# A gate matrix kept in HBM between two stages: its layout turned from piece first to group first

## The chip, the cores and the metric

The kernel runs on one core of one Trainium2 chip. The metric is the device time of one execution in microseconds (us); lower is better. The core has a matrix engine (PE), a vector engine (DVE), a scalar engine (ACT), GpSimd (POOL) and SyncE (SP), and sixteen DMA engines that all of them share. SP and ACT issue plain DMAs, each on a queue of its own (q1 is SP's, q10 is ACT's); POOL issues the indirect gathers (q0).

## The reference, cut to what matters

One encoder layer over 512 tokens of width 2048: attention and a recurrence, then a channel mixer (PEER) that picks, for each token, 16 experts from each of 8 heads out of 128 x 128 single-neuron experts. The change touches the mixer alone:

```python
out = lax.map(expert_chunk, ...)        # 128 tokens at a time
def expert_chunk(args):
    xc, ic, gc = args                   # tokens, 128 expert indices each, 128 gates each
    uc = u_emb[ic]
    act = jax.nn.gelu(jnp.einsum('cd,ced->ce', xc, uc))
    vc = v_emb[ic]
    return jnp.einsum('ce,ced->cd', (gc * act).astype(vc.dtype), vc)
```

## The kernel before, in words

176 of the 512 tokens are worked out by gathering rows of `u_emb` and `v_emb` (indirect DMAs on POOL, products on DVE, one "tick" at a time, spread over the whole mixer). The other 336 tokens (`TD`) are worked out densely: every expert's activation for every token, times a gate that is zero where the expert was not picked. The 16384 experts stand in 128 blocks (`NBLK`) of 128, one expert of a block to a partition.

The dense part has three steps.

- `u_block(b)` (lines 1118 to 1134) multiplies a block of `u_emb` with the tokens on PE (48 matmuls, in three products of high and low parts), takes the gelu on ACT into `ga`, 128 x 336, and stores most of these blocks to HBM (`ad`, line 1132). Its weights come as `raw` (1 MB by SP, line 255), are rounded to `hi` on ACT (line 269), and `lo = raw - hi` is made on DVE (line 281).
- While the first u blocks run, `g_step` builds the gates: 84 steps of four tokens, each a one-hot product on PE into `ps_G`, copied by ACT into `stg` (128 partitions x 128 blocks x 28 tokens, two buffers, line 1240). When 28 tokens (`TB`) are full, ACT writes the piece to the HBM matrix `gd` (line 1242): 12 pieces (`NTB`) in all, 14336 bytes of each partition.
- Later `load_g(g)` on SP (line 1341) reads back what a group of four blocks (`GRP`) needs, for all 336 tokens: 32 groups (`NG`), 5376 bytes of each partition. `weigh(b)` (lines 1343 to 1356) multiplies `ga` by its slice of `G` on DVE (line 1347), splits it into `Wh` and `Wl`, asks for the group after next, and reloads a stored `ga` as `gr` (line 1336, three buffers). `v_unit` then multiplies `Wh` and `Wl` with `v_emb` on PE (lines 1397 to 1399), eight blocks at a time; u blocks and v units alternate.

The order on every engine is written out by hand (`stage_plan`, `runs`); nothing is moved by a scheduler. An engine works through its instructions in order, and SP and ACT issue DMAs from the same streams, so a DMA that can't be issued yet holds up what stands behind it. Each DMA of SP and ACT counts its landing on one of eight counters (`DMAHW0` to `DMAHW7` in the built program), in turn; a DMA whose counter was last used by a transfer that may still be under way waits for that transfer first.

At one place ACT issues eight small loads in a row: `load_x` fetches the tokens of the last gather phase as `xng`, 16 partitions at a time (line 1148).

Of the kernel before, what the change touches and what calls it, by code (L numbers as in the profile page):

```python
# [8 lines left out]
F32 = mybir.dt.float32  # L9
# [21 lines left out]
NBLK = 128  # L31
GRP = 4
NG = NBLK // GRP
# [7 lines left out]
TB = 28  # L41
NTB = TD // TB
# [3 lines left out]
NB = 4  # L46
# [100 lines left out]
def tile_encoder(  # L147
# [24 lines left out]
    nc = tc.nc  # L172
    V, A, P, T = nc.vector, nc.scalar, nc.gpsimd, nc.tensor

    def pool(name, bufs=1, side="left", **kw):
        es = ExitStack()
        p = es.enter_context(tc.tile_pool(name=name, bufs=bufs, side=side, reuse_waits="tile", **kw))
        ctx.callback(es.close)
        return p, es.close
# [10 lines left out]
    psB = ctx.enter_context(tc.tile_pool(name="psB", bufs=2, space=PSUM))  # L190
    psC = ctx.enter_context(tc.tile_pool(name="psC", bufs=2, space=PSUM))
    dram = ctx.enter_context(tc.tile_pool(name="dram", bufs=1, space=DRAM))
    gd = dram.tile([128, NTB, NBLK, TB], F32, name="gd")
    x2d = dram.tile([DW, D], F32, name="x2d")
    x0d = dram.tile([128, D], F32, name="x0d")
    xnd = dram.tile([128 + NB1, D], F32, name="xnd")
# [461 lines left out]
    _, ps = next(gen)  # L658
# [160 lines left out]
    for c in range(4):  # L819
        ps = ps_l0 if c == 0 else [psA.tile([128, 512], F32, tag="A", name=f"ps_l{tt}") for tt in range(NT)]  # L820
# [391 lines left out]
    As, Bs, evac, gst = {}, {}, [], {}  # L1212
# [7 lines left out]
    def g_onehots(n):  # L1220

        if n < len(G_STEPS):
            tm, ta = G_STEPS[n]
            As[n] = g_one(lts[tm], ta, 0)
            if n % 2 == 0:
                V.tensor_tensor(As[n], As[n], lts[tm][:, 2, ta:ta + NB].unsqueeze(2).to_broadcast([128, NB, 128]),
                                op=ALU.mult)
        n -= 1
        if 0 <= n < len(G_STEPS):
            tm, ta = G_STEPS[n]  # L1230
            Bs[n] = g_one(lts[tm], ta, 1)
            if n % 2:
                for t in range(NB):
                    A.activation(out=As[n][:, t, :], in_=As[n][:, t, :], func=AF.Copy,
                                 scale=lts[tm][:, 2, ta + t:ta + t + 1])

    def flush_evac(keep=1):
        while len(evac) > keep:
            stg, o, ps, dst = evac.pop(0)
            A.copy(stg[:, :, o:o + NB], ps.rearrange("p t i -> p i t"))  # L1240
            if dst is not None:
                A.dma_start(out=dst, in_=stg)

    def g_step(n):
        flush_evac()
        g_onehots(n + G_AHEAD + 1)
        tt, ta = G_STEPS[n]
        B, Ao = Bs.pop(n), As.pop(n)
        at, o = divmod((tt - 1) * 128 + ta - NB1, TB)
        if o == 0:  # L1250
            gst["stg"] = gst["p"].tile([128, NBLK, TB], F32, tag="stg", name="stg")
        ps = psA.tile([128, NB, 128], F32, tag="A", name="ps_G")
        for t in range(NB):
            T.matmul(ps[:, t, :], B[:, t, :], Ao[:, t, :], start=True, stop=True)
        evac.append((gst["stg"], o, ps, gd[:, at] if o + NB == TB else None))

    def soft_b(t0):
        softmax_b(t0)
# [36 lines left out]
    def free_rt():  # L1295
# [6 lines left out]
    do = {"pair": lambda _: route_pair(), "sum": lambda _: route_sum(), "tr": lambda _: route_tr(), "sc": lambda _: route_sc(),  # L1302
          "pick": lambda _: route_pick(), "soft_a": lambda t: softmax_a(t, (1, 2, 4)[t]),
          "soft_b": soft_b, "free": lambda _: free_rt(), "g": g_step, "tick": lambda _: step(),
          "prime": lambda _: next(gg), "rep": lambda _: rep_lists(), "pre": g_onehots, "lists": lambda t: lts.update({t: g_lists(t)})}

    flush_lo()
    psS[:] = [psA, "A"]
    for b in range(lead0 - N_TRANS):
# [5 lines left out]

        u_block(b, hook)
    flush_evac(0)
    gst["close"]()
    gst["oh_close"]()
# [5 lines left out]
    gp, _ = pool("G", bufs=2)  # L1325
    grp, _ = pool("gr", bufs=3)
    acc = accp.tile([128, KD, TD], F32, name="acc")
    Gs, Ws = {}, {}
# [8 lines left out]

    def load_g(g):
        if g < NG:
            Gs[g] = gp.tile([128, NTB, GRP, TB], F32, tag="G", name="G")  # L1340
            nc.sync.dma_start(out=Gs[g], in_=gd[:, :, g * GRP:(g + 1) * GRP, :])

    def weigh(b):
        G, j = Gs[b // GRP], b % GRP
        ga = back_t.pop(b) if b in back_t else acts.pop(b)
        ga3 = ga.rearrange("p (a t) -> p a t", t=TB)
        V.tensor_tensor(ga3, ga3, G[:, :, j, :], op=ALU.mult)  # L1347
        Wh = wp.tile([128, TD], F32R, tag="Wh", name="Wh")
        Wl = wp.tile([128, TD], F32R, tag="Wl", name="Wl")
        A.copy(Wh, ga)  # L1350
        V.tensor_tensor(Wl, ga, Wh.bitcast(F32), op=ALU.subtract)  # L1351
        Ws[b] = Wh, Wl
        if j == GRP - 1:
            load_g(b // GRP + 2)
        if b in ad_at:
            reload()
# [21 lines left out]
    for i in range(N_TRANS):  # L1378
        ws = ((), (), (), range(3), range(3, 6), range(6, PR + LEAD))[i]
        u_block(lead0 - N_TRANS + i, beside=lambda: beside(ws))  # L1380
        if i == 0:
            for _ in range(3):
                reload()
        if i == 1:
            load_g(0)
            load_g(1)
# [205 lines left out]
```

## Time and profile before

| | |
|---|---|
| median of 3 runs | 2978.55 us (2971.44 to 2978.85) |
| the profiled execution | 2979.9 us, span 2978.1 us |
| PE busy in the span | 2849.8 us, 96% |
| DVE busy | 2321.1 us, 78% |
| ACT busy | 1145.4 us, 38% |
| DMA packets | 174624, of which 64096 are under 512 bytes |

"Busy" counts instructions of an engine from start to end; PE is busy nearly throughout, so what can be gained or lost shows in the time in which PE waits, stage by stage. The DMA share is the mean busy share of the sixteen DMA engines. The span is 1.8 us shorter than the time of the same execution.

### The profile page before, as it was taken

The numbers are of one execution on the slowest core, as the hardware profiler recorded it, in microseconds if no ns is written. First come the engines' busy times: TensorE is split into PE (matmuls) and PEld (weight loads), VectorE is DVE, ScalarE is ACT, GpSimd is POOL, SyncE is SP. The second block draws the span as 40 slices with busy tenths as digits, with TensorE's granted clock in tenths as the row PEclk, the third lists the DMA queues.
The fourth block names the chain that finished last, engine by engine and source line by source line (L and its number), as shares of the span: only waits on it lengthen the run. The fifth ranks groups of instructions, "written<-read, shape, count | busy, mean of one in ns | idle before, by whom it ended". The sixth has DMA issues, their size and how long they took to land. (4 is left out here: it accounts for less than half of the span.)

```text
span 2978.1 us, 41791 instructions
## 1 busy us (share of the span) xinstructions
PE 2849.8 (96%) x16945; PEld 2648.3 (89%) x16945; DVE 2321.1 (78%) x3206; ACT 1145.4 (38%) x1518; POOL 867.3 (29%) x562
## 2 busy tenths in 40 slices
PE   8999999999999999999999999999999999799997
PEld 6777867787889999998999999999999999799997
DVE  5773366544987899987888888888888888688885
ACT  6663254433444455543322232232333233232333
POOL 0000110001543422224343344344343433333322
PEclk9999999999999999999999999999999999999999
DMA  6222220233225798999999999999999999899983
GB/s 247 77 88 82 93 114 29 71 120 120 83 99 217 261 350 338 347 348 381 374 364 353 377 380 357 365 366 362 359 377 369 362 373 362 314 369 357 377 312 134
DMA packets 174624, 806.12 MB, mean 271 GB/s; under 512 B 64096, under 2 KB 82288, under 8 KB 83840
## 3 DMA queue, kind: packets, MB, share of 16 engines
q1 hardware_dynamic: 108096, 379.63, 34.4%
q0 software_dynamic: 52624, 379.42, 33.1%
q10 hardware_dynamic: 13712, 44.40, 4.0%
q8 instruction: 133, 2.18, 0.3%
q14 instruction: 59, 0.48, 0.0%
HBM read 759.33 MB, written 44.06 MB: 270 GB/s over the span
## 5 line engine op out<-in xcount | busy, mean ns | idle before, releaser
L281 DVE TENSOR_TENSOR lo<-raw,hi 128x2048 fp32r<-128x2048 f32 x316 | 724.4, 2293 | 380.9 <-ACT hi L269 379.6
L269 ACT CAST hi<-raw 128x2048 fp32r<-128x2048 f32 x316 | 603.4, 1910 | 739.2 <-PE ps_v L1398 464.0
L1399 PE MATMUL ps_v<-Wh,lo 128*128 128x336 f32 x2048 | 654.2, 319 | 26.5 <-DVE lo L281 26.5
L1397 PE MATMUL ps_v<-Wh,hi 128*128 128x336 f32 x2048 | 650.4, 318 | 20.4 <-DVE acc L1409 16.2
L299 PE MATMUL ps_u<-H,lo 128*128 128x336 f32 x2048 | 650.3, 318 | 10.1 <-DVE lo L281 10.0
L297 PE MATMUL ps_u<-H,hi 128*128 128x336 f32 x2048 | 653.5, 319 | 1.7 <-ACT hi L269 1.7
L1398 PE MATMUL ps_v<-Wl,hi 128*128 128x336 f32 x2048 | 650.8, 318 | 0.5
L298 PE MATMUL ps_u<-L,hi 128*128 128x336 f32 x2048 | 649.0, 317 | 0.0
L1154 POOL DMA_INDIRECT gv<-in_v_emb_dram,idx x176 | 351.3, 1996 | 582.1 <-DVE x L1181 426.3
L1154 POOL DMA_INDIRECT gu<-in_u_emb_dram,idx x176 | 333.5, 1895 | 631.4 <-DVE gu L1161 547.5
L1399 PEld LDWEIGHTS ps_v<-Wh,lo 128*128 128x128 f32 x2048 | 389.1, 190 | 29.4 <-DVE lo L281 29.3
L1397 PEld LDWEIGHTS ps_v<-Wh,hi 128*128 128x128 f32 x2048 | 389.5, 190 | 23.9 <-issue 18.3
L1161 DVE SCALAR_TENSOR_TENSOR gu<-gu,xng 128x2048 f32<-128x2048 f32 x176 | 400.8, 2283 | 2.4 <-DMA gu<-in_u_emb_dram,idx 2.4
L299 PEld LDWEIGHTS ps_u<-H,lo 128*128 128x128 f32 x2048 | 387.3, 189 | 12.6 <-DVE lo L281 12.6
L1398 PEld LDWEIGHTS ps_v<-Wl,hi 128*128 128x128 f32 x2048 | 389.1, 190 | 1.4 <-DVE Wl L1351 1.4
L297 PEld LDWEIGHTS ps_u<-H,hi 128*128 128x128 f32 x2048 | 387.7, 189 | 2.3 <-ACT hi L269 2.3
L298 PEld LDWEIGHTS ps_u<-L,hi 128*128 128x128 f32 x2048 | 387.6, 189 | 0.0
L1181 DVE SCALAR_TENSOR_TENSOR x<-gv,w,x 128x2048 f32<-128x2048 f32 x143 | 335.2, 2344 | 4.9 <-DMA gv<-in_v_emb_dram,idx 4.6
L1130 ACT ACTIVATE ga<-ps_u 128x336 f32<-128x336 f32 x128 | 57.5, 449 | 174.9 <-PE ps_u L299 174.4
L297 PE MATMUL ps_cm<-xh,hi 128*128 128x512 f32 x256 | 104.8, 409 | 11.5 <-ACT xh L368 9.2
L1409 DVE TENSOR_TENSOR acc<-ps_v,acc 128x336 f32<-128x336 f32 x240 | 109.6, 497 | 5.0 <-PE ps_v L1399 5.0
L1350 ACT CAST Wh<-gr 128x336 fp32r<-128x336 f32 x71 | 33.6, 473 | 193.8 <-DVE gr L1347 193.8
(321 smaller groups left out, 3678.5 us busy)
## 6 DMA issues: line engine op xcount, KB each, us to landing
raw<-in_u_t_dram SPq DMA_DIRECT2D x128, 1024.0 KB
raw<-in_v_t_dram SPq DMA_DIRECT2D x128, 1024.0 KB
raw<-in_w_dram SPq DMA_DIRECT2D x28, 1024.0 KB
gd<-stg ACTq DMA_DIRECT2D x12, 1792.0 KB
G<-gd SPq DMA_DIRECT2D x32, 672.0 KB
raw<-in_w_out_dram SPq DMA_DIRECT2D x16, 1024.0 KB
raw<-in_w_pq_dram SPq DMA_DIRECT2D x16, 1024.0 KB
ad<-ga ACTq DMA_DIRECT2D x71, 168.0 KB
```

What stands on the lines that cost most here:

```text
L269: A.copy(hi, raw)
L281: en.tensor_tensor(lo[:, c], raw[:, c], hi.bitcast(F32)[:, c], op=ALU.subtract)
L297: T.matmul(ps, ah, bh, start=first, stop=False)
L298: T.matmul(ps, ah, bl, start=False, stop=False)
L299: T.matmul(ps, al, bh, start=False, stop=last)
L1154: P.indirect_dma_start(out=g, out_offset=None, in_=u_emb if kind == "u" else v_emb, in_offset=bass.IndirectOffsetOnAxis(ap=ix, axis=0))
L1161: V.scalar_tensor_tensor(out=g, in0=g, scalar=1.0, in1=xs_t["x"], op0=ALU.mult, op1=ALU.mult, accum_out=a_t[h][:, k:k + 1])
L1181: V.scalar_tensor_tensor(out=d, in0=g, scalar=wk, in1=d, op0=ALU.mult, op1=ALU.add)
L1397: T.matmul(ps[:, 0:TD], hi[:, cc], Wh, start=j == 0, stop=False)
L1398: T.matmul(ps[:, 0:TD], hi[:, cc], Wl, start=False, stop=False)
L1399: T.matmul(ps[:, 0:TD], lo[:, cc], Wh, start=False, stop=j == PR - 1)
L1409: V.tensor_tensor(d, ps[:, 0:TD], d, op=ALU.add)
```

## The change

The HBM matrix `gd` has its axes in another order. Before, a partition's 14336 bytes of a piece were one run, and the 5376 bytes of a group were 12 runs of 448 bytes. Now a group's 5376 bytes are one run, and a piece goes into 32 runs of 448 bytes.

```diff
-    gd = dram.tile([128, NTB, NBLK, TB], F32, name="gd")
+    gd = dram.tile([128, NG, NTB, GRP * TB], F32, name="gd")
...
             if dst is not None:
-                A.dma_start(out=dst, in_=stg)
+                A.dma_start(out=dst, in_=stg.rearrange("p (g j) t -> p g (j t)", j=GRP))
...
-        evac.append((gst["stg"], o, ps, gd[:, at] if o + NB == TB else None))
+        evac.append((gst["stg"], o, ps, gd[:, :, at, :] if o + NB == TB else None))
...
-            Gs[g] = gp.tile([128, NTB, GRP, TB], F32, tag="G", name="G")
-            nc.sync.dma_start(out=Gs[g], in_=gd[:, :, g * GRP:(g + 1) * GRP, :])
+            Gs[g] = G = gp.tile([128, NTB, GRP, TB], F32, tag="G", name="G")
+            nc.sync.dma_start(out=G.rearrange("p a j t -> p (a j t)"), in_=gd[:, g].rearrange("p a f -> p (a f)"))
```

The tiles in SBUF keep their shapes, and no instruction of PE, DVE or POOL moves. On ACT, where a piece has been filled in the g steps, the issue stands at the same place and has another shape (`hi` is the rounded weight, `ohA` a one-hot operand):

```order
 L269 CAST hi<-raw 128x2048
 L1240 COPY stg<-ps_G 128x128x4
-L1242 DMA gd<-stg 128x3584
+L1242 DMA gd<-stg 4096x1x112
 L1234 ACTIVATE ohA<-ohA,lt 128x128 x4
 L1240 COPY stg<-ps_G 128x128x4 x2
```

One issue of 128 rows of 3584 elements has become one of 4096 rows of 112 elements; nothing around it moved. On SP, where the dense part changes from u blocks alone to u blocks and v units, the first loads of `G` stand among the weight loads and the reloads of `ga`:

```order
 L1336 DMA gr<-ad 128x336 x3
 L255 DMA raw<-in_u_t_dram 128x2048
-L1341 DMA G<-gd 128x12x112 x2
+L1341 DMA G<-gd 128x1344 x2
 L255 DMA raw<-in_v_t_dram 128x2048 x2
 L1336 DMA gr<-ad 128x336 x3
 L255 DMA raw<-in_v_t_dram 128x2048
-L1341 DMA G<-gd 128x12x112
+L1341 DMA G<-gd 128x1344
```

Again the shape alone differs. On ACT at the eight `xng` loads, with the counters that an issue waits for, four of the waits stay as they were and one is new, on the second load:

```order
-L1148 DMA xng<-xnd 16x2048 x4
+L1148 DMA xng<-xnd 16x2048
+L1148 DMA xng<-xnd 16x2048 [waits DMAHW5_49]
+L1148 DMA xng<-xnd 16x2048 x2
 L1148 DMA xng<-xnd 16x2048 [waits DMAHW0_49]
 L1148 DMA xng<-xnd 16x2048 [waits DMAHW1_49]
 L1148 DMA xng<-xnd 16x2048 [waits DMAHW2_49]
 L1148 DMA xng<-xnd 16x2048 [waits DMAHW3_49]
```

In both programs `DMAHW2` was last used by the `G` load that SP issues just before these loads, `DMAHW1` by the weight load ahead of it, and `DMAHW5`, in the changed program, by the `G` load of the group before that.

## Rows read from the trace of the kernel before

**Rows 1.** Page, part 1: busy us, share of span, instructions by engine
```profile
PE 2849.8 (96%) x16945; PEld 2648.3 (89%) x16945; DVE 2321.1 (78%) x3206; ACT 1145.4 (38%) x1518; POOL 867.3 (29%) x562
```

**Rows 2.** Windows by stage: length, PE, PEld, DVE, ACT, POOL busy, PEclk, DMA, GB/s
```profile
1050.00:1320.00 270.00, 257.10 (x1818) 255.00 (x1817) 260.13 (x278) 143.68 (x284) 63.91 (x41) 0.99 0.91 343
1340.00:2065.00 725.00, 688.11 (x4374) 681.16 (x4373) 616.47 (x553) 223.21 (x211) 285.49 (x135) 0.98 0.97 367
2065.00:2490.00 425.00, 423.75 (x2766) 423.50 (x2765) 372.70 (x315) 131.96 (x113) 165.84 (x85) 1.00 0.96 369
2490.00:2600.00 110.00, 95.06 (x609) 94.81 (x608) 81.97 (x70) 29.83 (x26) 37.67 (x19) 0.94 0.91 333
```

**Rows 3.** Waits, 1330 to 2110 us: total us, times, longest us
```profile
PE ps_v L1399 <- DVE lo L281: 26.5, 10, 4.0
...
DVE gr L1347 <- DMA gr<-ad: 18.3, 9, 2.7
```

**Rows 4.** DMA, 1617 to 1618 us: packets by size, then q1's packets, MB, share
```profile
DMA packets 699, 0.34 MB, mean 340 GB/s; under 512 B 674, under 2 KB 698, under 8 KB 698
...
q1 hardware_dynamic: 692, 0.32, 111.5%
```

**Rows 5.** DMA, 1060 to 1067 us: q10 with one write to gd
```profile
q10 hardware_dynamic: 144, 1.84, 61.3%
```

**Rows 6.** DMA, 1082.7 to 1088.4 us: q10 with the next write to gd
```profile
q10 hardware_dynamic: 139, 1.84, 88.8%
```

**Rows 7.** Issues of gd's loads and writes: duration ns min/median/max, first and last start
```profile
L1341 SPq DMA_DIRECT2D G<-gd x32: 529/530/4172, 1334.5 to 2778.3; - x32
L1242 ACTq DMA_DIRECT2D gd<-stg x12: 326/326/327, 1056.4 to 1317.9; - x12
```

**Rows 8.** Timeline of SP at two places: start us, length us, issue
```profile
1334.49 5.20 SPq L1341 DMA_DIRECT2D G<-gd  x2
1339.79 8.13 SPq L255 DMA_DIRECT2D raw<-in_v_t_dram  x2
...
1610.80 0.53 SPq L1341 DMA_DIRECT2D G<-gd  x1
1611.84 4.89 SPq L1336 DMA_DIRECT2D gr<-ad  x1
```

**Rows 9.** Timeline of ACT at two of the twelve writes
```profile
1174.55 0.33 ACTq L1242 DMA_DIRECT2D gd<-stg  x1
...
1175.46 0.33 ACTq L1132 DMA_DIRECT2D ad<-ga  x1
1175.83 1.92 ACT L269 CAST hi<-raw 128x2048 fp32r<-128x2048 f32 x1 [0.40 <-ACT ga L1130]
...
1198.18 0.33 ACTq L1242 DMA_DIRECT2D gd<-stg  x1
1208.33 0.33 ACTq L1132 DMA_DIRECT2D ad<-ga  x1
```

**Rows 10.** Timeline of DVE at the first of these writes
```profile
1178.60 2.28 DVE L281 TENSOR_TENSOR lo<-raw,hi 128x2048 fp32r<-128x2048 f32 x1
```

**Rows 11.** Timelines of SP, ACT and DVE at the xng loads, then PE's longest wait
```profile
2526.30 0.53 SPq L1341 DMA_DIRECT2D G<-gd  x1
...
2550.79 1.30 ACTq L1148 DMA_DIRECT2D xng<-xnd  x2
2552.19 1.90 ACT L269 CAST hi<-raw 128x2048 fp32r<-128x2048 f32 x1 [22.55 <-issue]
...
2554.12 2.29 DVE L281 TENSOR_TENSOR lo<-raw,hi 128x2048 fp32r<-128x2048 f32 x1 [17.51 <-ACT hi L269]
...
PE ps_v L1397 <- DVE acc L1409: 14.9, 1, 14.9
```

**Rows 12.** DMA, 2537.6 to 2548.4 us, by queue
```profile
q0 software_dynamic: 426, 3.15, 80.0%
q1 hardware_dynamic: 732, 0.33, 15.4%
```

## The prediction

> **What bounds the kernel now.** I read the page's busy times first. PE is busy for 2849.8 of 2978.1 us [rows 1], so about 128 us is all that any change of transfers can give back, and more can be lost. The windows by stage show where those us lie. While the gates are built and written, 1050 to 1320 us, PE is busy for 257 of 270 us and DVE for 260: both are nearly full, and the DMA engines have a share of 0.91. From 1340 to 2065 us, where `G` is read and `ga` is reloaded, PE misses 37 us and DMA is at 0.97. From 2065 to 2490 us `G` is still read by the same small runs, DMA is at 0.96, and PE misses 1.3 us. From 2490 to 2600 us PE misses 15 us [rows 2]. So a slow `G` load alone costs nothing: the waits belong to the reloads and to one place near 2550 us.
>
> Then the waits. In the read stage PE waits 26.5 us for `lo`, because DVE, which makes it, waits 18.3 us in nine pieces for `gr` [rows 3]. At 2550 us the chain is longer, and starts at a `G` load. SP issues it at 2526.3. ACT's last two `xng` issues come out only at 2550.79, and `hi`, which stands behind them in ACT's stream, starts at 2552.19 after 22.55 us without work; DVE's `lo` waits 17.51 us for that `hi`, and PE 14.9 us for DVE [rows 11]. The issue that is let go at 2550.79 is the one that waits for `DMAHW2`, the `G` load's counter.
>
> **What the change removes and adds.** The count of 448-byte packets stays the same: 32 loads x 1536 = 49152 before, 12 writes x 4096 = 49152 after. They move from SP's queue to ACT's, and from the read stage to the write stage.
>
> *Price of a packet.* In the one us in which nearly only `G` packets ran, q1 took 111.5% of 16 engines for 692 packets: 17.84 us / 692 = 25.8 ns each [rows 4]. A write to `gd` is 128 packets of 14336 bytes: 61.3% of 16 x 7 us over at most these is 536 ns each, 4.3 us of all sixteen engines [rows 5]; the next took 88.8% of 16 x 5.7 us, 5.1 us [rows 6]. No row shows a 448-byte write; the reads of that size are the nearest rows, and I take their price. A write then costs 4096 x 25.8 / 16 = 6.6 us, 1.9 more than the mean of 4.7, or 23 us for twelve. A `G` load costs 2.5 us now; as 128 packets of 5376 bytes, by bytes at 536 ns for 14336, 201 ns each, 1.6 us. That is 0.9 less, 28 us for 32.
>
> *Gain at 2550 us: 11 us, plus 1.* Between 2537.6 and 2548.4 us q0 moved 426 packets and q1 732 [rows 12], so in ten us the `G` load passed less than half of its 1536 small packets: it gets about one or two turns for each gather packet of 8192 bytes. With 128 packets instead of 1536 it needs a twelfth of these turns and should land before 2540 us. ACT is then let go some 11 us earlier. The bounds are 0 (another of the eight waits takes over) and 14.9. One us more comes back because the granted clock, 0.94 of the 2.4 GHz level in this stretch [rows 2], falls around such a wait. The Trainium skill says the same of the turns ("DMA: Bandwidth & Descriptors", Queues, rings and completion order: each DMA engine goes round its queues packet by packet); the count in rows 12 agrees.
>
> *Gain in the read stage: 5 us.* After a `G` load the next issue on SP is held: 4.89 us behind one [rows 8], where an issue of 128 rows takes 0.33. That hold goes, since 8 packets an engine replace 96. But the reload that DVE waits for mostly stands ahead of the `G` load in SP's stream, behind a 1 MB weight load, and the stage stays full of gathers. I give back 0.9 us less DMA work at about half a dozen of the stalls. Bounds: 0, and the 18.3 us of the nine waits.
>
> *Loss on ACT in the write stage: 17 us.* The write puts 256 packets on each engine where a `G` load put 96. Behind one `G` load the next issue came out 5.9 us after the load's own issue (1610.80 to 1616.73); with two `G` loads in a row the second was itself held (4172 ns instead of 530, [rows 7]), and the weight load behind them came out some 13 us after the first issue [rows 8]. So the issue of `gd` may pass, but the next one on ACT, `ad<-ga`, will be held until part of the 256 packets has gone. ACT's queue has no weight loads ahead of it: the last 160 packets an engine are 160 x 25.8 ns = 4.1 us, and with the start of the transfer at least 5 us; the two loads in a row, scaled to 256 packets, give 17 us. I take 8, nearer to the emptier queue. In the twelve writes `ad` comes from 0.91 us (the issue at 1174.55) to 10.15 us (at 1198.18) behind `gd` [rows 9]; taking 8 less each gap, the holds add up to 25 us. Behind `ad` stands `hi`, and DVE, which is full, takes up `lo` as little as 0.85 us after `hi` has ended (1177.75 to 1178.60, [rows 9, 10]). After the slack of each block some 17 us are left as DVE waits. Bounds by the same sum: 5 us of waits at 5 us a write, 70 at 13.
>
> *Loss to full DMA engines: 5 us.* Twelve writes add 23 us to a stage whose engines are idle for 0.09 x 270 = 24 us [rows 2]. It just fits; gathers and weights are asked for early, so I charge a fifth. Bounds 0 and 23. The last write lands later too; SP's first reload waits for it, and the two `G` loads behind, no longer held for 5.20 us [rows 8], give that back.
>
> **Sum.** -11 - 1 - 5 + 17 + 5 = +5 us on the profiled execution's 2979.9, so 2985. That execution lies 1.4 us above the median of the runs shown, which gives 2983.5 there; I say 2984. A difference under 0.3%, 9 us, can't be told from none.
>
> **Rivals.**
> - *The writes are hidden: 2963.* If ACT's queue takes 256 packets an engine without holding the next issue, only the gains remain: 2980 - 17. For it: every `gd` issue now takes 326 ns and none is held [rows 7]. Against it: the same queue type on SP does hold. It decides when `ad` still takes 0.33 us.
> - *ACT is held by the write itself: about 3010.* If the issue of `gd` can't complete until its packets fit, as the second `G` load's did not [rows 7], ACT loses 6 to 7 us at each of twelve places, of which it now idles about half before the next `hi`; the same sum gives 22 to 45 us of DVE waits instead of 17.
> - *Small writes cost more than small reads: about 3040.* If each 448-byte write takes twice its 25.8 ns, a write costs 13 us, DMA work grows by 12 x 8.5 = 100 us where 24 are free, and the stage lengthens by some 75 us; less the gains, 60 remain. In the trace nothing speaks for it and nothing excludes it. The Trainium skill gives such a rule ("DMA: Bandwidth & Descriptors", Specifications: 512 bytes are the least for full rate, and below it the DMA engine reads, modifies and writes); no run here shows a write that small. By that rule, this rival is the outcome.
> - *In between: about 2995.* Write packets of 30 to 36 ns add 14 to 31 us to a DMA stage that is then over-full.
>
> **How the numbers follow.** The sum as it stands, within 9 us of before: 0.32. Hidden writes, or a larger gain at the reloads: 0.24. ACT held by the write itself: 0.18. Dearer writes in between: 0.14. Twice the price: 0.12. So faster 0.24, same 0.32, slower 0.44. The range runs from 2957 (both gains near their bounds, no loss) to 3040 (the third rival), and leaves out about 2 in 10. The likeliest case alone: 2970 to 2989.
>
> **What would show it.** In the profile after: `ad<-ga` issues longer than 0.33 us behind `gd` show the hold, a `gd` issue of several us shows the second rival, and q10's share over one write shows the packet's price. DVE's busy time from 1050 to 1320 us and the waits of `lo` for `hi` there show what the holds cost. No issue on SP held behind a `G` load, and PE's 14.9 us wait cut to about 4, show the gains. The prediction is wrong if small writes have another price than small reads, or if the hold isn't set by packets that are still queued.

## The result and the profile after

The changed kernel takes 2995.28 us (median; 2994.4 to 3006.51 in 4 runs), the kernel before 2977.03 us on the same chip: a ratio of 1.0075, 95% interval 1.006 to 1.009, so 18 us slower. The profiled execution of after is the longest of its four (3006.51 us; the others lie between 2994.4 and 2995.75), so sums of its trace come out some 11 us above the medians.

The windows by stage, with the columns of [rows 2], of the kernel after:

```profile
1050.00:1320.00 270.00, 240.36 (x1629) 235.58 (x1627) 238.95 (x258) 129.07 (x259) 51.20 (x36) 0.96 0.91 305
1340.00:2065.00 725.00, 690.26 (x4392) 682.92 (x4391) 612.28 (x538) 223.00 (x207) 280.92 (x135) 0.98 0.96 369
2065.00:2490.00 425.00, 420.07 (x2723) 419.55 (x2722) 369.71 (x317) 132.34 (x118) 167.30 (x84) 0.99 0.94 363
2490.00:2600.00 110.00, 99.70 (x634) 99.45 (x633) 87.04 (x73) 31.50 (x30) 42.31 (x20) 0.94 0.95 340
```

The loss is in the first line, where the gates are written: PE is busy for 17 us less than in [rows 2] and DVE for 21 us less, POOL for 13 us less, and the clock is at 0.96 instead of 0.99, while the DMA share, 0.91, is the same: the DMA engines have not become fuller, and PE and DVE wait for something else. The read stage gains 2 us of PE and the place at 2550 us 4.6. The windows stand at the same times in both traces, and behind the write stage the work comes some 28 us later in this one, so what a stage loses at its end can fall into the next. Of the 3.7 us that the third line loses, most is such a shift: PE's last wait of the read stage, 2.8 us for `lo`, ends at 2089.36 us, where one of 3.2 ended at 2061.48 before. The rest belongs to a wait that ends at 2371.97 us, 2.1 us where it was 1.3.

The issues of the writes, of `G` and of `ad` (duration ns min/median/max, first and last start), after:

```profile
L1242 ACTq DMA_DIRECT2D gd<-stg x12: 520/521/582, 1053.2 to 1344.5; - x12
L1341 SPq DMA_DIRECT2D G<-gd x32: 319/386/606, 1364.2 to 2804.8; - x32
L1132 ACTq DMA_DIRECT2D ad<-ga x71: 321/326/10008, 880.0 to 2004.6; - x71
```

No write is held when it is issued, and no `G` load is held any more (4172 ns at most in [rows 7]). From the first to the last write 291.3 us pass; before it was 261.5 us (1056.4 to 1317.9, [rows 7]). And one `ad`, 168 KB, took 10 us to issue. The timeline of ACT around it, after, and DVE's and PE's at the same place:

```profile
1181.55 0.53 ACTq L1242 DMA_DIRECT2D gd<-stg  x1
1182.18 0.45 ACT L1130 ACTIVATE ga<-ps_u 128x336 f32<-128x336 f32 x1 [0.66 <-ACT stg L1240]
1182.67 10.01 ACTq L1132 DMA_DIRECT2D ad<-ga  x1
1192.72 1.90 ACT L269 CAST hi<-raw 128x2048 fp32r<-128x2048 f32 x1 [10.08 <-issue]
```
```profile
1194.65 2.29 DVE L281 TENSOR_TENSOR lo<-raw,hi 128x2048 fp32r<-128x2048 f32 x1 [8.96 <-ACT hi L269]
```
```profile
1194.67 0.65 PE L297 MATMUL ps_u<-H,hi 128*128 128x336 f32 x1 [5.10 <-ACT hi L269]
1195.11 0.48 PE L298 MATMUL ps_u<-L,hi 128*128 128x336 f32 x1
1196.99 0.65 PE L299 MATMUL ps_u<-H,lo 128*128 128x336 f32 x1 [1.40 <-DVE lo L281]
```

This is the whole chain in one place: the write passes in 0.53 us, the small `ad` behind it stands for 10 us, `hi` behind `ad` comes after 10.08 us without work ("issue": ACT waited for nothing but its own stream), DVE stands 8.96 us and PE 5.10 and 1.40 us. PE then pays again. In these windows (columns as before) its granted clock is 0.50 and 0.54, the 1.2 GHz level, after the wait, and 1.00 before it and eight us later:

```profile
1180.00:1189.50 9.50, 9.50 (x68) 9.29 (x66) 5.65 (x8) 1.97 (x6) 1.16 (x1) 1.00 1.08 302
1194.60:1199.00 4.40, 2.94 (x9) 2.51 (x10) 4.35 (x2) 4.00 (x9) 0.00 (x0) 0.50 0.31 51
1199.00:1203.00 4.00, 4.00 (x17) 4.00 (x16) 3.96 (x7) 2.11 (x6) 1.16 (x1) 0.54 0.98 377
1203.00:1207.00 4.00, 4.00 (x34) 4.00 (x33) 4.00 (x4) 1.51 (x4) 2.19 (x1) 1.00 0.38 160
```

In four us at 0.54 PE begins 17 matmuls, at 1.00 it begins 34. So, by an estimate from these counts, a 5 us wait costs some 4 us more: in the 8.4 us after it PE begins 26 matmuls, which take 3.1 us at the rate of 34 in four us, and waits 1.4 us.

`ad` is held by over 2 us behind seven of the twelve writes between 1084 and 1323 us (6.95, 6.16, 3.97, 10.01, 6.62, 7.60 and 6.18 us) and behind the last one, at 1350.42 (9.02 us), together 56.5 us. The waits from 1050 to 1345 us, after (total us, times, longest):

```profile
ACT hi L269 <- issue: 48.0, 7, 10.1
DVE lo L281 <- ACT hi L269: 33.6, 8, 9.0
```

In the kernel before, no `ad` was held, and `lo` waited 9.0 us for `hi` in three pieces (1050 to 1330 us):

```profile
L1132 ACTq DMA_DIRECT2D ad<-ga x71: 326/326/333, 883.2 to 1977.9; - x71
DVE lo L281 <- ACT hi L269: 9.0, 3, 6.1
```

### The profile page after: what moved, and what is told of

Same layout as the page of the kernel before. It is cut to its first block, busy times and chain, and to the rows that moved or that the text cites. A ratio compares the mean times of both kernels' runs of the same rounds, so it can differ in the third digit from the quotient of the medians.

```text
span 3004.7 us, 41792 instructions
## 1 busy us (share of the span) xinstructions
PE 2861.9 (95%) x16945; PEld 2658.0 (88%) x16945; DVE 2321.8 (77%) x3206; ACT 1144.9 (38%) x1518; POOL 863.9 (29%) x562
## 3 DMA queue, kind: packets, MB, share of 16 engines
q10 hardware_dynamic: 61328, 44.40, 5.2%
## 5 line engine op out<-in xcount | busy, mean ns | idle before, releaser
L1399 PE MATMUL ps_v<-Wh,lo 128*128 128x336 f32 x2048 | 654.8, 320 | 24.6 <-DVE lo L281 24.6
L297 PE MATMUL ps_u<-H,hi 128*128 128x336 f32 x2048 | 657.9, 321 | 13.1 <-ACT hi L269 13.1
L297 PEld LDWEIGHTS ps_u<-H,hi 128*128 128x128 f32 x2048 | 391.1, 191 | 14.9 <-ACT hi L269 14.8
L1350 ACT CAST Wh<-gr 128x336 fp32r<-128x336 f32 x71 | 33.6, 473 | 186.3 <-DVE gr L1347 186.3
```

What stands on the lines that cost most here:

```text
L297: T.matmul(ps, ah, bh, start=first, stop=False)
L1399: T.matmul(ps[:, 0:TD], lo[:, cc], Wh, start=False, stop=j == PR - 1)
```

## The experiments

All times are medians; each ratio is against the kernel before, run beside it, which took 2975.86 us beside the first four kernels (the table of two by two, the writes on SP, the write in four), 2974.99 beside the next four and 2976.73 beside the last three. In the expectations H stands for the hold on ACT's queue as the cause, D for the time that the packets take of the DMA engines.

**Two by two: the length of the runs on each side.** The first kernel is the kernel before, and reads a run of 5376 bytes:

```diff
-            nc.sync.dma_start(out=Gs[g], in_=gd[:, :, g * GRP:(g + 1) * GRP, :])
+            nc.sync.dma_start(out=Gs[g].rearrange("p a j t -> p (a j t)"),
+                              in_=gd.rearrange("p a b t -> p (a b t)")[:, g * NTB * GRP * TB:(g + 1) * NTB * GRP * TB])
```

> The gate matrix is written as before, in one run of 14336 bytes, and read as one run of 5376 bytes of the same memory. The elements of G so stand in the wrong places, and only the time is read. It is the change's gain without its price. Both theories (H: ACT's queue is held behind the 256 small packets an engine of a write; D: the small packets cost DMA time in a stage that is full) expect the write stage as before, no issue of ad longer than 0.33 us, and the gain that the changed kernel shows after 1340 us: some 3 us in the read stage and 5 at the xng loads, so about 2969 us, 0.997 of before. If the read half were worth the 17 us that I forecast, it would be 2960.

The second is the changed kernel, and reads 12 runs of 448 bytes:

```diff
-            nc.sync.dma_start(out=G.rearrange("p a j t -> p (a j t)"), in_=gd[:, g].rearrange("p a f -> p (a f)"))
+            nc.sync.dma_start(out=G, in_=gd.rearrange("p g a f -> p (g a f)").rearrange("p (a b t) -> p a b t", a=NTB, t=TB)[:, :, g * GRP:(g + 1) * GRP, :])
```

> The piece is written in 32 runs of 448 bytes as in the changed kernel, and read in 12 runs of 448 bytes as before, from the same memory. The elements of G so stand in the wrong places, and only the time is read. It is the price without the gain. Both H and D expect the whole loss of the write stage, some 28 to 31 us in the profile, and no gain afterwards: 3003 to 3010 us, 1.009 to 1.011 of before, slower than the changed kernel.

| write | read in runs of 448 | read in runs of 5376 |
|---|---|---|
| runs of 14336 | 1 (before) | 0.9974 [0.9962, 0.9986], 2968.89 us |
| runs of 448 | 1.0101 [1.0073, 1.0128], 3003.23 us | 1.0075 [1.006, 1.009] (after) |

Both columns and both rows agree. Short writes cost 27 us with short reads (3003.23 - 2975.86) and 26 with long ones (2995.28 - 2968.89); long reads give back 7 to 8 us (2975.86 - 2968.89, and 0.0026 of the time, 7.7 us, between the ratios of either row). That is the change taken apart: -7 or -8, and +26.

**The hold, or the packets?** If ACT's stream is what suffers, the same packets from another queue must cost nothing. The changed kernel with its writes on SP's queue:

```diff
-                A.dma_start(out=dst, in_=stg.rearrange("p (g j) t -> p g (j t)", j=GRP))
+                nc.sync.dma_start(out=dst, in_=stg.rearrange("p (g j) t -> p g (j t)", j=GRP))
```

> The changed kernel with the write to gd issued by SP in place of ACT. H: ACT's queue has only ad on it and is never held; the hold moves to SP, where the weight loads stand that are asked for two blocks ahead, so the write stage comes within 10 us of before, 2970 to 2982 us in all. If the weight loads have less room than that, they come late, hi waits for raw, and the loss stays. D: same packets, same DMA time: 2990 to 3000 us.

2969.19 us, 0.9982 [0.9968, 0.9995]: all of the 26 us have gone, and the time is that of the first kernel of the table. It lies just under the 2970 to 2982 us of H and far from the 2990 to 3000 of D. Its window, and DVE's wait from 1050 to 1345 us (12.3 us in the kernel before):

```profile
1050.00:1320.00 270.00, 257.31 (x1816) 255.21 (x1815) 260.14 (x276) 142.74 (x281) 63.74 (x40) 0.99 1.01 342
```
```profile
DVE lo L281 <- ACT hi L269: 13.4, 6, 5.6
```

The DMA share is 1.01 (0.91 in [rows 2], 0.92 in the first kernel of the table), and PE and DVE are as busy as in [rows 2]. SP's weight loads are now held behind the writes, by up to 5.8 us, and no `hi` waits for its `raw` in this window. So full DMA engines aren't the cause, nor the price of a packet.

The other way round: the writes stay on ACT, and only `ad`, the instruction that was held, goes to SP.

```diff
-            A.dma_start(out=ad[ad_at[b]], in_=ga)
+            nc.sync.dma_start(out=ad[ad_at[b]], in_=ga)
```

> The changed kernel with ad issued by SP and the write to gd left on ACT. On ACT's queue nothing then stands behind a write until the next write 22 us later. H, as I hold it: the write's own issue passes in some 0.52 us and only the next issue on the same queue is held, so ACT is never held and the loss of the write stage goes: 2965 to 2975 us. If a write in flight slows ACT or DVE itself (its 256 packets an engine read SBUF in small runs), the loss stays: 2985 to 2995. The ad issues can't be held by weight loads of 8 packets an engine, but SP may now wait for ga, and then weight loads come later.

2966.23 us, 0.9969 [0.9959, 0.998]. Issues of the writes and of `ad`, and window in this kernel:

```profile
L1242 ACTq DMA_DIRECT2D gd<-stg x12: 520/521/587, 1046.6 to 1307.9; - x12
L1132 SPq DMA_DIRECT2D ad<-ga x71: 320/327/1102, 877.7 to 1962.5; - x71
```
```profile
1050.00:1320.00 270.00, 257.41 (x1813) 255.32 (x1812) 259.30 (x272) 138.16 (x273) 63.14 (x40) 0.99 1.01 347
```

ACT issues the same twelve writes of 4096 packets, from the first to the last in 261.3 us again, and without a second DMA close behind them nothing on ACT is held. With the kernel above this settles the mechanism: the loss needs a small write and another DMA after it in the same stream. It also answers a rival, that `ad` stands for one of the eight counters, as I take an `xng` load to do at 2550 us. The counters go round the DMAs of SP and ACT in turn, and neither edit changes the order of the DMAs in the kernel, yet `ad` takes 1.1 us at most here and 0.33 us with the writes on SP.

**The dose.** A write in four issues of 1024 runs, one a g step:

```diff
-                A.dma_start(out=dst, in_=stg.rearrange("p (g j) t -> p g (j t)", j=GRP))
+                src = stg.rearrange("p (g j) t -> p g (j t)", j=GRP)
+                for h in range(0, NG, 8):
+                    wq.append((dst[:, h:h + 8, :], src[:, h:h + 8, :]))
+        for _ in range(min(len(wq), 1 if keep else len(wq))):
+            o_, i_ = wq.pop(0)
+            A.dma_start(out=o_, in_=i_)
```

> The changed kernel with each write to gd cut into four issues of 1024 runs of 448 bytes, one after each of the next four g steps. The same packets, the same bytes, the same engine and queue, but never more than some 64 new packets an engine at a time. H: the holds of ad go (from 56 us in eight places to a few us), and with them most of the loss: the write stage within 8 us of before, 2970 to 2980 us in all. D: the packets take the same DMA time as in the changed kernel, so the write stage stays about as long and the time stays within 5 us of the changed kernel's 2995.

2984.5 us, 1.0028 [1.0013, 1.0043]: 11 us better than after (14 by the ratios), and a miss: H had expected 2970 to 2980, D about 2995. The holds are spread out, and the writes themselves take part in them (issues of this kernel):

```profile
L1249 ACTq DMA_DIRECT2D gd<-stg x48: 366/398/4354, 1055.6 to 1330.0; - x48
L1132 ACTq DMA_DIRECT2D ad<-ga x71: 326/327/6920, 882.3 to 1981.2; - x71
```

Runs of 896 bytes, 16 a partition, so half as many packets a write; `G` is read in runs of 5376 of the same memory, and its elements stand in the wrong places (the write and the read change with the tile):

```diff
-    gd = dram.tile([128, NG, NTB, GRP * TB], F32, name="gd")
+    gd = dram.tile([128, NG // 2, NTB, 2 * GRP * TB], F32, name="gd")
...
-                A.dma_start(out=dst, in_=stg.rearrange("p (g j) t -> p g (j t)", j=GRP))
+                A.dma_start(out=dst, in_=stg.rearrange("p (g j) t -> p g (j t)", j=2 * GRP))
...
```

> The changed kernel with a piece written in 16 runs of 896 bytes in place of 32 of 448, by ACT as before: 128 packets an engine for each write, not 256. The memory is ordered by groups of eight blocks and still read in runs of 5376 bytes, so the elements of G stand in the wrong places, and only the time is read. H with a limit near 100 packets, as the holds behind one G load of 96 suggest: only some 30 packets have to go before the next issue passes, so only the four writes with ad less than 4 us behind are held, the loss is under 10 us and the time 2970 to 2978. If the hold is simply in proportion to the packets, half the loss stays: 2980 to 2985. D, a price per packet in a full stage, was against the run with the write on SP already; it would also say half the loss.

2978.31 us, 1.0004 [0.9993, 1.0015], just above the 2970 to 2978 that I expected. `ad` is held three times by over a us, by 3.3 us at most:

```profile
ACT hi L269 <- issue: 8.3, 3, 3.4
L1242 ACTq DMA_DIRECT2D gd<-stg x12: 520/521/582, 1056.0 to 1320.2; - x12
```

8.3 us in place of 48.0, and 264.2 us from the first to the last write. With the bytes unchanged, it is the count of packets that holds the queue. Half the packets give a sixth of the hold, but that does not show a threshold, as my expectation had it: a hold that ends in half the time, behind an `ad` that comes 1 to 10 us after the write, leaves less than half the wait. Halving the eight times from write to release of the changed kernel (9.4 to 16.8 us) and taking off each gap leaves 10 us, near what is seen, so the two can't be told apart here. Some 9 us stay against the first kernel of the table; the write stage is 2.7 us longer than in the kernel before, so most of them lie elsewhere and weren't traced.

**The place at 2550 us.** ACT stands there at its `xng` issues, and I took the reason to be that one of them waits for a counter. The same loads issued by SP, in two kernels: the one with the writes on SP, and the kernel before.

```diff
-                    A.dma_start(out=t[n * q:n * (q + 1)], in_=xnd[r0:r0 + n, :])
+                    nc.sync.dma_start(out=t[n * q:n * (q + 1)], in_=xnd[r0:r0 + n, :])
```

> The run with the write on SP (2969 us), and also the twelve late xng loads issued by SP in place of ACT. If PE's 10.8 us wait near 2550 us comes from ACT standing at the xng issue whose counter the G load holds, SP stands there instead, hi passes, and that wait goes, with about 3 us of the wait near 2338 us: 2954 to 2962 us. If the wait comes from the full DMA engines in that stretch (weights or gathers late), it stays and the time is 2966 to 2972.

> The kernel before with the twelve late xng loads issued by SP, and nothing else: G is still read in runs of 448 bytes. If the G load's slow landing costs PE only through ACT, the 14.9 us wait goes without any change to gd: 2958 to 2966 us. If the small packets themselves keep weights away in that stretch, PE still waits there, and the time is 2970 or more.

2960.22 us (0.9944 [0.9927, 0.996]) and 2965.79 us (0.9962 [0.9948, 0.9976]): 9 us each, against the kernel with the writes on SP (11 by the ratios) and against the kernel before. PE's longest wait from 2490 to 2600 us in the second, the kernel before with that edit alone:

```profile
PE ps_v L1397 <- DVE acc L1409: 3.0, 1, 3.0
```

It was 14.9 us [rows 11], with the same `G` load in the same small runs. So the wait belonged to ACT's place in the line, and a shorter `G` load is only one way to shorten it.

**Is the layout worth anything without its cost?** `ad` and `xng` both on SP, with the changed layout, then with the old one, and `ad` alone on SP with the old one:

> The changed kernel with `ad` and the late `xng` loads issued by SP, the writes to `gd` left on ACT. If the two ACT waits are the whole of the story, the gains of both edits add up: 2966 from `ad` on SP alone, and about as much again as the `xng` edit gave where it was tried (9 us each time), so 2957. If the granted clock or the full DMA engines take part of it back, 2961 to 2966.

> The kernel before with the same two edits, so that the layout alone differs from the run above. If the new layout is worth the 3 us of the read stage once its cost on ACT is gone, this one is 3 to 6 us slower than the run above (2960 to 2963). If the layout is worth nothing then, both give the same time. If `ad` on SP gains by itself, both lie lower than the sum of the parts says.

> The kernel before with `ad` alone on SP. In the kernel before, no `ad` was held behind a write by more than the time in which ACT's queue takes its 128 packets an engine, and `lo` waited 9 us for `hi` in the write stage. If those waits come from the writes, this gives up to 9 us (2966 to 2970), and the gain of the same edit in the changed kernel was that of the layout only for the rest. If it gives nothing (2973 to 2977), the whole of the changed kernel's recovery was its own hold.

| | old layout | changed layout |
|---|---|---|
| `ad` on SP | 2966.33 us, 0.9967 [0.9957, 0.9978] | 2966.23 us, 0.9969 [0.9959, 0.998] |
| `ad` and `xng` on SP | 2956.01 us, 0.9928 [0.9911, 0.9945] | 2955.82 us, 0.993 [0.9907, 0.9953] |

Here my expectation of 3 to 6 us for the layout was a miss: no difference is seen, though the intervals are wide enough (5 to 7 us in the lower row) that one of 3 us can't be excluded. And `ad` on SP gains 10 us in the old kernel too, where no `ad` was held. It isn't the writes: `lo` waits as long for `hi` in the write stage as before (8.9 us, 1050 to 1320 us), and the stage takes 261.4 us against 261.5, first to last write. In the trace of the old layout with `ad` on SP:

```profile
L1132 SPq DMA_DIRECT2D ad<-ga x71: 326/327/1702, 877.0 to 1964.2; - x71
L1242 ACTq DMA_DIRECT2D gd<-stg x12: 326/326/327, 1045.8 to 1307.2; - x12
```

From the first `ad` to the first write 168.8 us pass in place of 173.2 (883.2 to 1056.4), 4.4 us less, and from the last write to the end of the span 1655.3 in place of 1660.2, 4.9 us less. Part of that is the issue itself. In the kernel before, `hi` starts 0.86 us after `ga` does (956.25 to 957.11 us), with an issue of 0.33 us between them; with `ad` alone on SP and the old layout the two stand 0.35 us apart:

```profile
947.84 0.45 ACT L1130 ACTIVATE ga<-ps_u 128x336 f32<-128x336 f32 x1
948.19 1.89 ACT L269 CAST hi<-raw 128x2048 fp32r<-128x2048 f32 x1
```

Half a us at each of 71 stores on a chain that PE often waits for can give such a sum; how much of the 10 us it is, wasn't measured by itself. So of the 29 us that `ad` on SP gives the changed kernel (2995.28 to 2966.23), 10 come with either layout, and 19 take away the whole of what the layout had cost, gains counted in. That the 7 us of the long reads don't show here as they do with the writes on SP may have a place, the start of the read stage. SP's first reload waits there for the landing of the last write (1300 to 1345 us), and DVE for the first `G` (1325 to 1400 us), in the kernel with the changed layout and `ad` on SP, then in that with the old layout:

```profile
SPq L1336 <- DMA gd<-stg: 13.7, 1, 13.7
DVE gr L1347 <- DMA G<-gd: 9.9, 1, 9.9
```
```profile
SPq L1336 <- DMA gd<-stg: 5.1, 1, 5.1
DVE gr L1347 <- DMA G<-gd: 0.7, 1, 0.7
```

The small runs land later: with `ad` and `xng` on SP a write takes 20.1 us to land (median; 14.6 to 27.3) in the changed layout and 9.2 (6.7 to 13.1) in the old one. DVE's wait follows that only loosely, though. With the writes on SP it is 1.4 us in one kernel and 7.6 in the one with `xng` on SP too, and in the kernel before with `xng` on SP 5.8. At the place near 2550 us the changed layout still gives some 5 us (PE's wait of 10.4 against 15.4 us in these two). That the two cancel is an argument from these traces and not shown: no run here takes that first wait away by itself.

## Why the prediction was right in its range and wrong in its terms

I forecast 2984 us, some 5 above the median that I had (2978.55), with no change that can be told as the likeliest single case (0.32) and slower (0.44 in three cases) ahead of faster (0.24). It became 2995.28, 18 us slower. That is inside the range, which is 83 us wide, but 11 us above the sum. The mechanism of the largest term was right and is shown. Two sizes were off, both to the same side: the losses were put at 22 us and are 26 to 27, the gains at 17 and are 7 to 8. It was luck that the losses came so near: the 5 us charged for full DMA engines stand for nothing, and made up for half of what the hold was short by.

- *What bounds it.* Right. The loss fell where DVE and PE were nearly full, the gains at the reloads and at 2550 us.
- *Price of a packet, 25.8 ns.* Nearly right. In the page of before q10 has 13712 packets, 12 x 128 of them of 14336 bytes [rows 5, 6], and 4.0% of the span; in the page of after it has 61328 and 5.2%. Before, that is 0.040 x 16 x 2978.1 = 1906 us of packet time, of which 1536 x 0.536 = 823 us are the long writes and 1083 the rest; after, 0.052 x 16 x 3004.7 = 2500 us, and (2500 - 1083) / 49152 = 29 ns are left for a small write; the shares are rounded, which is worth a ns. In two windows of the trace of after, 1054 to 1062 and 1183 to 1190 us, q10 takes 43.9% of 16 engines for 2247 packets, 25.0 ns each, and 87.9% for 2891, 34.1 ns. So the doubling of my third rival isn't seen. The Trainium skill's rule beside which that rival stood ("DMA: Bandwidth & Descriptors", Specifications: below 512 bytes the DMA engine reads, modifies and writes) gives no price; no run here shows a doubling, nor whether such a write is read first.

```profile
q10 hardware_dynamic: 13712, 44.40, 4.0%
```
```profile
q10 hardware_dynamic: 61328, 44.40, 5.2%
```
```profile
q10 hardware_dynamic: 2247, 1.01, 43.9%
```
```profile
q10 hardware_dynamic: 2891, 1.30, 87.9%
```

- *The hold on ACT, 17 us.* Right in kind: the write passes, `ad` is held, `hi` and `lo` are late. The size was wrong. I let the queue take on `ad` 8 us after the write's issue; it took 9.4 to 16.8 us in the eight places where it was held, 12.3 in the mean, halfway between my 8 and the 17 that two `G` loads in a row gave by scaling. So the holds add up to 56.5 us and not 25, and DVE's waits for `hi` rose by 24.6 us (33.6 - 9.0), not by 17; the 9.9 us behind the last hold, after 1345 us, come on top. The packets that have to go first were counted about right, 160 an engine or 2560: at the release q10 had moved 2543 to 3309 of the write's 4096 in seven of the eight places, and 4026 in one. What failed is the time for them, 4.1 us at the full rate of sixteen engines, from which I went up to 8. I chose the emptier queue, but until the release gathers and weights shared the engines, and q10 had 30 to 62% of them. In three of the four places without a hold `ad` came 7.4 to 8 us behind the write, q10 had had 83 to 98%, and 3444 to 4092 packets had gone. One place of each kind, from the write's issue to the release (1127.90 to 1137.25 us), and to the issue of `ad` (1102.50 to 1109.96 us):

```profile
q10 hardware_dynamic: 2919, 1.31, 53.1%
```
```profile
q10 hardware_dynamic: 3444, 1.54, 98.2%
```

  And I left out the clock, which I had counted at 2550 us: behind six of the eight holds the granted clock fell to between 0.50 and 0.73 over some four us, behind two (3.97 and 6.18 us) it didn't.
- *Full DMA engines, 5 us.* Wrong. The share went to 1.01 with the writes on SP at no cost that can be seen; this term is nothing.
- *Gain at 2550 us, 11 + 1 us.* Mis-sized: PE's wait fell from 14.9 to 10.3 us, 4.6. SP, ACT and PE there, after:

```profile
2556.62 0.42 SPq L1341 DMA_DIRECT2D G<-gd  x1
```
```profile
2558.07 19.70 ACTq L1148 DMA_DIRECT2D xng<-xnd  x7
2577.87 1.90 ACT L269 CAST hi<-raw 128x2048 fp32r<-128x2048 f32 x1 [17.91 <-issue]
```
```profile
PE ps_v L1397 <- DVE acc L1409: 10.3, 1, 10.3
```

  `hi` starts 21.3 us after the issue of `G`, before 25.9. The step that failed is "a twelfth of these turns": it counted turns and took their length as fixed. From 2562 to 2572 us, after:

```profile
q0 software_dynamic: 140, 1.02, 46.7%
q1 hardware_dynamic: 140, 0.69, 28.6%
q10 hardware_dynamic: 138, 0.55, 24.9%
```

  Three queues take turns one for one, and each turn of q1 lasts 16 x 10 / 140 = 1.14 us on an engine. The Trainium skill says the same of the turns ("DMA: Bandwidth & Descriptors", Queues, rings and completion order). Before, by [rows 12], a turn was 16 x 10.8 / 732 = 0.24 us. A twelfth of the turns at almost five times the length is no twelfth of the time. But the longer turn is not that of the longer packet alone. In the kernel before, from 2532 to 2536 us, while ACT's queue still had `xng` packets, q1 passed its 448-byte packets in turns of 16 x 4 / 67 = 0.96 us:

```profile
q0 software_dynamic: 72, 0.59, 69.1%
q10 hardware_dynamic: 70, 0.27, 29.4%
q1 hardware_dynamic: 67, 0.03, 6.4%
```

  [rows 12] begin behind that stretch, so their mean turn was the wrong one to count with. How little the count of packets shortens a load shows over all 32 of them too, in the kernels with `ad` and `xng` on SP, first with the old layout, then with the changed one (us from the issue of a `G` load to its landing). A load of a twelfth of the packets lands 1.4 us sooner in the median:

```profile
DMA to landing us min/median/max: 6.3/10.9/18.2
```
```profile
DMA to landing us min/median/max: 5.6/9.5/14.7
```

- *Gain in the read stage, 5 us.* It is some 3, by difference: 7 to 8 in all, less 4.6 at 2550 us. DVE's waits for `gr` went from 18.3 us [rows 3] to

```profile
DVE gr L1347 <- DMA gr<-ad: 13.1, 8, 2.3
```

  and PE's for `lo` only from 26.5 to 24.6 us.
- *The rivals.* "ACT is held by the write itself" is refuted by issues of 0.52 us, "hidden" by the 56.5 us, "twice the price" by 29 ns. "In between" had the time, 2995, and with 30 ns nearly the price, for a reason that is not the one: its over-full DMA stage costs nothing when the writes come from SP.

Open stays what makes the count at the release differ from one write to the next (2543 to 4026 packets), and why `ad` on SP gains as much as 10 us in the kernel before, of which the write stage has none.

## What to carry to other kernels

Count packets where they are issued: a layout that moves small runs from one queue to another moves the hold with them, to whatever stands behind them in that engine's stream. Before turning a layout round, look at what the issuing engine does next; a store or load moved to an engine whose stream has room (`ad` and `xng` to SP) ended 21 us below the kernel before with either layout, and the layout gave nothing on top that can be seen. Price a queue's packets by the share of the engines that it gets beside the others, and not at their full rate. And price a wait on PE with the slow clock that follows it.

## What the hardware showed that I had not expected

- A DMA of 4096 packets (256 on each engine) passes ACT in 0.52 us, and the one behind it, 128 packets, stands up to 10 us; with 128 packets an engine it stands 3.3 us at most.
- Writes of 448 bytes to HBM cost 25 to 34 ns each, about what reads of that size cost (25.8), and a DMA share of 1.01 over 270 us went with no loss.
- A `G` load of 128 packets, 0.7 MB, still took some 20 us from its issue to the release of ACT, beside two queues that took a turn for each of its own.
